# Neighbourhood attention in an encoder trunk: one unit of work per head instead of two

## The chip, the cores and the metric

The kernel runs on one core of one Trainium2 chip, in one launch. The metric is the device time of that launch in microseconds (us). The core's engines work side by side and each takes its own instructions strictly in order: PE does matrix products (its weight loads are listed apart as PEld), DVE does elementwise work and reductions, ACT does activation functions and scaled copies, POOL a few small powers and some transfers, SP issues nearly all DMA transfers. Products are written to PSUM, which has eight banks of 512 float32 columns for 128 partitions. Everything else lies in SBUF.

## The reference

The program computes two layers of an encoder trunk on one sequence of 512 tokens (8 rows by 64 columns of a grid) with 1024 features in float32. Each layer mixes tokens in three parallel ways, merges them with sigmoid gates, and follows with a SwiGLU block and a gated embedding. Only the third mixer is touched by the change:

```
def neighbourhood_attention(qc, kc, vc, rpb):          # 8 heads of 64 features
    R = S // GRID_W                                    # 8 rows, 64 columns
    cs = clip(cols - NA_KC // 2, 0, GRID_W - NA_KC)    # each query sees 16 columns ...
    col_idx = cs[:, None] + arange(NA_KC)[None, :]
    def row(args):
        ...                                            # ... of all 8 rows
        s = einsum('bhwd,bhrwcd->bhwrc', q_r, kn) * DC ** -0.5
        s = s + bias
        a = softmax(s.reshape(B, HC, GRID_W, KR * NA_KC), axis=-1)
        return einsum('bhwrc,bhrwcd->bhwd', a, vn)
```

## The kernel before

**Layout.** Tokens are reordered so that the eight rows of one grid column lie together. A block of 128 queries then needs only a short run of keys: the four query blocks of a head see the key runs `KEYS = ((0, 192), (64, 256), (192, 256), (320, 192))` (first key, count). What lies in a run but outside a query's window is masked by a bias of -1e30, which comes with the position bias as a ready table from memory.

**Precision.** Every float32 operand of a product is split into a high and a low part (`split`: an ACT copy gives the high part, a DVE subtraction the low one), and a plain product is issued three times (`mm3`, lines L178 to L180). Queries and keys of the neighbourhood heads are stacked so that two products per score tile are enough (L803). Probabilities are split after their transposition (lines of `split` with tile `pt` and `a`), and the value matrix already carries its high and low halves side by side in 128 columns per head, so a value product gives two halves of 64 rows that are added at the end.

**Order of the work.** PE's instructions run in the order in which the Python program emits them. The large projections are walked in chunks of three products of 512 columns; every fourth chunk calls `tick`, which resumes the small generators that wait (`live`) and starts at most one new one from a queue (`later`, with a delay and a gap before the next start). So a neighbourhood unit is cut by its `yield`s into steps, and each step is put between two groups of twelve wide products. The other engines' instructions are put in order by a scheduler from priorities; `high_priority(offset=n)` moves an instruction up by n places. Weights are loaded by SP into three buffers (`wr`, L172), split by ACT and DVE into `wh` and `wl`, and used by PE.

**A unit before.** `natten_in` makes queries and keys of two heads (`pr` is the pair) and queues four units: (half 0, head 0), (half 0, head 1), (half 1, head 0), (half 1, head 1), one tick apart. A unit (`natten_unit`) covers two of the four query blocks of one head:

1. One bias tile `b` of 128 by 2 by 256 is loaded by SP (L704, two buffers). Two score tiles of 192 and 256 columns are made in one PSUM bank each (L803, tag `sc`, two banks). DVE adds the bias, negates and takes the row minimum in one instruction that writes back into `b` (L713); ACT takes exponentials from `b` into a tile `e` with the row sum (tag `e`, four buffers); DVE takes reciprocals (L721); ACT scales both `e` tiles in place.
2. After two ticks PE transposes four blocks into one bank (L729, tag `tr`, two banks); three of them are split into `pt` (128 by 384), the fourth, which has 64 keys only, into `a`.
3. After two more ticks PE makes the value products: two of 256 columns (L743), two of 128 (L745), one of 128 (L746), in a bank with tag `av` for the first head and `mm` for the second. ACT and DVE split the result into `y` and add its halves.

The three projections `glu`, `diff` (the first mixer, differential attention, whose units use the same `sc`, `tr`, `av` banks and `e`, `pt`, `a` tiles) and `gatec` run between and after these units. `conv` taps fill DVE in the background.

Of the kernel before, what the change touches and what calls it, by code (L numbers as in the profile page):

```python
# [20 lines left out]
P = 128  # L21
L = 2
# [6 lines left out]
HC = 8  # L29
# [2 lines left out]
HALO = CON3W // 2  # L32
NA_KR = 8
NA_KC = 16
NW = 256
KEYS = ((0, 192), (64, 256), (192, 256), (320, 192))
PLE = 256
DFF = 2816
# [5 lines left out]
FILL = -1.0e30  # L44
# [8 lines left out]
ORDER = (0, 2, 4, 6, 1, 3, 5, 7)  # L53
GAP = 144
HIGH = 200
BACC = dict(dynamic_dma_scratch_size=1024)


# [4 lines left out]
class Net:  # L63
# [315 lines left out]
    def small(self):  # L379

        for tag in ("ident", "ones"):
            self.sb(tag, [P, P], bufs=1)
        for tag in ("onesr", "zeror"):
            self.sb(tag, [P, P], F32R, bufs=1)
        for tag, n in (("b", 2 * NW), ("s", 10), ("sm", 8), ("rc", 4)):
# [214 lines left out]
    def values(self, ap, parts):  # L600


        mm = self.nc.tensor.matmul
        accs = [self.ps("mm", (P, 2, 256)) for _ in range(2)]
        for o in range(0, KD, 4):
            wh, wl = self.weights(ap[:, o * 256:(o + 4) * 256], 1024)
            both = [(k, t) for k in range(o, o + 4) for t in range(4)]
            if o == 0:

                both.sort(key=lambda kt: kt[1] // 2)  # L610
            for n, (k, t) in enumerate(both):
# [6 lines left out]
                mm(out, self.h[k][:, 0, ts], wl[:, s], start=False, stop=False,  # L618
                   skip_group_check=True)
                mm(out, self.h[k][:, 1, ts], wh[:, s], start=False,  # L620
                   stop=k == KD - 1 and t % 2 == 1, skip_group_check=True)
                if n % 2:
                    self.chunk()
        vs = []
        for acc in accs:
            v = self.sb("v", [P, 2, 512], F32R)
            for t in range(2):
                for hi, lo, a in parts(v[:, t], acc[:, t]):
                    self.split(hi, lo, a)
            vs.append(v)  # L630
        return vs

    def natten_in(self, pr, st, ys):
# [63 lines left out]
    def natten_unit(self, pr, half, u, st4, k2, st, y):  # L697

        nc, i = self.nc, self.i
        mm = nc.tensor.matmul  # L700
        head = 2 * pr + u
        b = self.sb("b", [P, 2, NW])
        with self.tc.high_priority(offset=100):
            nc.sync.dma_start(b, self.a["bias"][i, head, half])  # L704
        es = []
        m = self.sb("s", [P, 6])
        for t in range(2):
            qt = 2 * half + t
            k0, n = KEYS[qt]
            sc = self.ps("sc", (P, n))  # L710
            self.scores(sc, st4, k2, u, slice(qt * P, (qt + 1) * P), slice(k0, k0 + n))
            with self.tc.high_priority(offset=min(HIGH, self.tc.cur_priority - self.p0)):
                nc.vector.tensor_tensor_reduce(  # L713
                    out=b[:, t, :n], in0=sc, in1=b[:, t, :n], scale=-1.0, scalar=3.0e38,
                    op0=ALU.add, op1=ALU.min, accum_out=m[:, t:t + 1])
            e = self.sb("e", [P, n])
            self.act(e, b[:, t, :n], AF.Exp, table="exp", scale=-1.0, bias=m[:, t:t + 1],
                     accum_out=m[:, 2 + t:3 + t])
            es.append(e)
        with self.tc.high_priority(offset=min(HIGH, self.tc.cur_priority - self.p0)):  # L720
            nc.vector.reciprocal(m[:, 4:6], m[:, 2:4])  # L721
        for t, e in enumerate(es):
            self.act(e, e, AF.Copy, scale=m[:, 4 + t:5 + t])
        yield 2
        pt = self.ps("tr", (P, 4, P))
        p2 = self.sb("a", [P, P], F32R)
        outer, inner = es[half], es[1 - half]
        near, far = (64, 0) if half == 0 else (0, P)
        turn = lambda out, a: nc.tensor.transpose(out, a, self.ident)  # L729
        turn(pt[:, half], outer[:, near:near + P])  # L730
        turn(pt[:, 1 - half], inner[:, half * P:half * P + P])
        turn(pt[:, 2], inner[:, P - half * P:2 * P - half * P])
        turn(pt[:64, 3], outer[:, far:far + 64])
        pp = self.sb("pt", [P, 2, 512], F32R)[:, :, :3 * P]
        self.split(pp[:, 0], pp[:, 1], pt[:, :3].rearrange("p a b -> p (a b)"))
        self.split(p2[:64], p2[64:], pt[:64, 3])
        yield 2
        vs = st["v"]
        av = self.ps(("av", "mm")[u], (P, 256))
        cols = slice(head * P, head * P + P)  # L740
        at = lambda t: slice(t * P, (t + 1) * P)
        for k in range(2):
            mm(av, vs[2 * half][:, cols], pp[:, k, :256], start=k == 0, stop=False)  # L743
        for k in range(2):
            mm(av[:, at(1 - half)], vs[1][:, cols], pp[:, k, 256:], start=False, stop=False)  # L745
        mm(av[:, at(half)], vs[3 + half][:, cols], p2, start=False, stop=True)  # L746


        qs = slice(half * 256, half * 256 + 256)
# [635 lines left out]
def _bias_tiles(rpb):  # L1385
    t = np.arange(S)
    w, r = t // GR, t % GR
    cs = np.clip(w - NA_KC // 2, 0, GW - NA_KC)
    out = np.full((L, HC, 4, P, NW), FILL, dtype=rpb.dtype)
    for qt in range(4):  # L1390
        q = np.arange(qt * P, (qt + 1) * P)
        k0, n = KEYS[qt]
        k = np.arange(n) + k0
        ro = r[k][None, :] - r[q][:, None] + NA_KR - 1
        co = w[k][None, :] - w[q][:, None] + NA_KC - 1
        ok = (w[k][None, :] >= cs[q][:, None]) & (w[k][None, :] < cs[q][:, None] + NA_KC)
        out[:, :, qt, :, :n] = np.where(
            ok, rpb[:, :, np.where(ok, ro, 0), np.where(ok, co, 0)], out[:, :, qt, :, :n])
    out = out.reshape(L, HC, 2, 2, P, NW).transpose(0, 1, 2, 4, 3, 5)
    return np.ascontiguousarray(out)  # L1400


# [7 lines left out]
def _layout(v):  # L1410
# [4 lines left out]
    for i in range(L):  # L1415
# [44 lines left out]
```

## Time and profile before

| | us |
|---|---|
| Median of three runs | 1774.33 (1773.85 to 1774.78) |
| Profiled execution, its own time | 1775.07 |
| Its span, first to last instruction | 1773.3 |
| PE busy | 1763.5 |
| PE weight loads busy | 1555.2 |
| DVE busy | 1420.0 |
| ACT busy | 891.2 |
| POOL busy | 98.4 |

The profile is of one execution. Its span lies 1.77 us under that execution's own time, and that time lies 0.74 us over the median. Products are pipelined and the end of each is modelled, so PE is shown busy nearly always; what PE really spends on a product is read from the distance between the starts of two successive products, which the timeline gives. A row such as `natten_e<-natten_b,natten_s 128x256 f32` names the tile written, the tiles read and the shape; a bracket at the end of a timeline row gives the idle time before the instruction and what ended it. The units of this change run in two stretches, from 79.8 us to about 180 us in the first layer and from 958.5 us to about 1060 us in the second.

### The profile page before, as it was taken

To read this page: it belongs to the slowest core of one execution; us is meant where nothing else is said; L and a number is where in the kernel's file an instruction comes from. 1 tells how busy PE (TensorE), PEld (TensorE's weight loads), DVE (VectorE), ACT (ScalarE), POOL (GpSimd) and SP (SyncE) were. 2 spreads that over 40 slices of the span, in tenths; PEclk is the share of its full clock that TensorE was granted. 3 is DMA by queue.
4 is the path that set the end of the run, shared out by engine and by line. 5 is a ranking of instruction groups with operands and counts; after the bars stand their busy time and mean duration, and the time that the engine had idled before them with its cause. 6 is when DMAs were issued, how large, how long until landed. Compare 5 with 4: busy or idle time off the path is not lost.

```text
span 1773.3 us, 27306 instructions
## 1 busy us (share of the span) xinstructions
PE 1763.5 (99%) x10178; PEld 1555.2 (88%) x10178; DVE 1420.0 (80%) x2418; ACT 891.2 (50%) x1561; POOL 98.4 (6%) x114
## 2 busy tenths in 40 slices
PE   9999999999999999999999999999999999999998
PEld 7888888888899899998888888888888998989987
DVE  7977987998798587787777779889887975867776
ACT  5576555225565254454545755452356643534444
POOL 0000000000111010100000000000001110101000
PEclk9999999999999999999999999999999999999999
DMA  5666541334757366544446755423256664656332
GB/s 207 171 192 172 161 125 43 113 99 140 228 152 189 115 166 160 136 125 128 139 127 188 189 155 149 113 72 96 92 176 201 173 179 113 176 136 159 99 104 95
DMA packets 112548, 255.00 MB, mean 144 GB/s; under 512 B 14368, under 2 KB 19232, under 8 KB 112416
## 3 DMA queue, kind: packets, MB, share of 16 engines
q1 hardware_dynamic: 99024, 228.88, 42.2%
q0 software_dynamic: 12672, 23.07, 8.2%
q8 instruction: 80, 1.31, 0.3%
q10 hardware_dynamic: 720, 1.31, 0.2%
q14 instruction: 52, 0.43, 0.1%
HBM read 215.46 MB, written 7.34 MB: 126 GB/s over the span
## 4 chain that ended last, share of the span: by engine, by line
PE 86%; DVE 6%; ACT 3%; DMA 3%; issue 1%; SPq 0%; POOL 0%; ACTq 0%; DVEq 0%; POOLq 0%
PE ffn_mm L1009 4%; PE ffn_mm L1011 4%; PE ffn_mm L178 4%; PE ffn_mm L179 4%; PE ffn_mm L180 4%; PE ffn_mm L1010 4%; PE ffn_sc L1011 3%; PE ffn_sc L1009 3%; PE ffn_sc L1010 3%; PE mergea_mm L178 2%; PE mergea_mm L180 2%; PE mergea_mm L179 2%; PE gateb_mm L179 2%; PE gateb_mm L178 2%; PE gateb_mm L180 2%; PE wo_mm L178 2%
## 5 line engine op out<-in xcount | busy, mean ns | idle before, releaser
L161 DVE SCALAR_TENSOR_TENSOR conv_z<-glu_z,pre_par,conv_z 128x512 f32<-128x512 f32 x240 | 179.5, 748 | 3.5
L144 ACT ACTIVATE ffn_wh<-ffn_wr 128x1024 fp32r<-128x1024 f32 (+1 forms) x92 | 92.7, 1014 | 111.4 <-PE ffn_mm L179 74.7
L979 POOL DMA_DIRECT2D ffn_qk<-w_fu x88 | 78.1, 989 | 604.8 <-DMA ffn_qk<-w_fu 368.2
L158 DVE TENSOR_TENSOR ffn_wl<-ffn_wr,ffn_wh 128x1024 fp32r<-128x1024 f32 (+1 forms) x92 | 107.3, 1172 | 5.4 <-ACT ffn_wh L144 4.9
L158 DVE TENSOR_TENSOR ffn_t<-ffn_mm,wo_rb 128x512 f32<-128x512 f32 (+1 forms) x64 | 38.6, 604 | 67.9 <-PE ffn_mm L180 67.9
L144 ACT ACTIVATE mergea_wh<-mergea_wr 128x1024 fp32r<-128x1024 f32 (+1 forms) x32 | 27.1, 846 | 96.8 <-PE mergea_mm L179 79.5
L144 ACT ACTIVATE ffn_wh<-ffn_qk 128x1024 fp32r<-128x1024 f32 x44 | 46.7, 1060 | 36.1 <-PE ffn_mm L179 16.0
L158 DVE TENSOR_TENSOR ffn_wl<-ffn_qk,ffn_wh 128x1024 fp32r<-128x1024 f32 x44 | 53.8, 1223 | 10.7 <-ACT ffn_wh L144 10.7
L158 DVE TENSOR_TENSOR ffn_t<-ffn_t,ffn_t 128x512 f32<-128x512 f32 (+1 forms) x46 | 31.3, 680 | 32.1 <-ACT ffn_t L144 31.5
L144 ACT ACTIVATE diff_a<-diff_sc,diff_s 128x512 f32<-128x512 f32 x32 | 22.0, 688 | 61.1 <-DVE diff_s L894 61.1
L178 PE MATMUL ffn_mm<-ffn_v,ffn_wh 128*128 128x512 f32 x132 | 51.4, 389 | 0.0
L179 PE MATMUL ffn_mm<-ffn_v,ffn_wh 128*128 128x512 f32 x132 | 51.4, 389 | 0.0
L180 PE MATMUL ffn_mm<-ffn_v,ffn_wl 128*128 128x512 f32 x132 | 51.3, 389 | 0.0
L178 PE MATMUL ffn_mm<-ffn_y,ffn_wh 128*128 128x512 f32 x132 | 51.3, 389 | 0.0
L179 PE MATMUL ffn_mm<-ffn_y,ffn_wh 128*128 128x512 f32 x132 | 51.3, 389 | 0.0
L180 PE MATMUL ffn_mm<-ffn_y,ffn_wl 128*128 128x512 f32 x132 | 51.3, 389 | 0.0
L1010 PE MATMUL ffn_sc<-wo_h,ffn_wh 128*128 128x256 f32 x176 | 49.8, 283 | 0.0
L1011 PE MATMUL ffn_sc<-wo_h,ffn_wl 128*128 128x256 f32 x176 | 49.8, 283 | 0.0
L1010 PE MATMUL ffn_mm<-wo_h,ffn_wh 128*128 128x256 f32 x176 | 49.8, 283 | 0.0
L1011 PE MATMUL ffn_mm<-wo_h,ffn_wl 128*128 128x256 f32 x176 | 49.8, 283 | 0.0
L1009 PE MATMUL ffn_sc<-wo_h,ffn_wh 128*128 128x256 f32 x176 | 49.8, 283 | 0.0
L1009 PE MATMUL ffn_mm<-wo_h,ffn_wh 128*128 128x256 f32 x176 | 49.8, 283 | 0.0
(879 smaller groups left out, 6569.4 us busy)
## 6 DMA issues: line engine op xcount, KB each, us to landing
ffn_qk<-w_fu POOLq DMA_DIRECT2D x88, 256.0 KB, 5.9
ffn_wr<-w_fg SPq DMA_DIRECT2D x44, 512.0 KB, 3.7
ffn_wr<-w_fd SPq DMA_DIRECT2D x32, 448.0 KB, 4.0
ffn_r<-w_fu SPq DMA_DIRECT2D x44, 256.0 KB, 4.0
ffn_qk<-w_fg SPq DMA_DIRECT2D x44, 256.0 KB, 4.3
ffn_qk<-w_fu SPq DMA_DIRECT2D x44, 256.0 KB, 4.5
natten_wr<-w_in SPq DMA_DIRECT2D x16, 512.0 KB, 4.3
natten_b<-bias SPq DMA_DIRECT2D x32, 256.0 KB, 4.0
```

The costliest lines, as they stand in the source:

```text
L144: i = self.nc.scalar.activation(out, in_, func, **kw)
L158: return self.nc.vector.tensor_tensor(out, a, b, op)
L161: return self.nc.vector.scalar_tensor_tensor(out, a, s, b, op0, op1)
L178: mm(out, wh, ah, start=first, stop=False)
L179: mm(out, wh, al, start=False, stop=False)
L180: mm(out, wl, ah, start=False, stop=last)
L979: nc.gpsimd.dma_start(q, wu[:, lo], accum_op=ALU.add)
L1009: mm(out, wh[:, c], bh, start=first and k == 0, stop=False, skip_group_check=True)
L1010: mm(out, wh[:, c], bl, start=False, stop=False, skip_group_check=True)
L1011: mm(out, wl[:, c], bh, start=False, stop=k == 3, skip_group_check=True)
```

## The change

A unit now covers a whole head. Two units per pair are queued instead of four, with a gap of two ticks.

- **Scores.** The two score tiles of a half share one bank of 448 columns (192 and 256). All four tiles' products of a head are emitted one half after the other, eight products in a row.
- **Softmax in place.** The bias tiles are now two per head, 128 by 448, held in the tags `e` and `b` by turns (six buffers in all). The exponentials and the scaled probabilities overwrite them; no separate `e` tile is used. One reciprocal serves all four tiles.
- **Transposes.** After `WAIT` = 3 ticks (2 before) eight transposes run in a row into both `tr` banks. Their splits are one of 128 by 512, one of 128 by 256 and one of 64 by 256, moved up by 20 places (`SOON`).
- **Values.** After `VALW` = 2 ticks: six products of 256 columns and two of 128, all into one bank of 512 columns. The middle value block, which before met each half in 128 columns, meets both halves at once (columns 128 to 384).
- **Result.** `y` is split and added in one pass of 512 columns instead of two of 256.

```
-        for n in range(4):
-            self.later(self.natten_unit(pr, n // 2, n % 2, st4, k2, st, ys[pr]), 6 if pr == 3 else 5 if pr else 11, 1)
+        for u in range(2):
+            self.later(self.natten_unit(pr, u, st4, k2, st, ys[pr]), 6 if pr == 3 else 5 if pr else 11, 2)
...
+        ahead = lambda: self.tc.high_priority(offset=min(HIGH, self.tc.cur_priority - self.p0))
+        sooner = lambda: self.tc.high_priority(offset=min(SOON, self.tc.cur_priority - self.p0))
+        bs = [self.sb(("e", "b", "e")[(2 * head + half) % 3], [P, NW]) for half in range(2)]
         with self.tc.high_priority(offset=100):
-            nc.sync.dma_start(b, self.a["bias"][i, head, half])
+            for half, b in enumerate(bs):
+                nc.sync.dma_start(b, self.a["bias"][i, head, half])
...
+        for half, b in enumerate(bs):
+            both = self.ps("sc", (P, NW))
+            ...
+                for a, keys in enumerate((st4[:, 2 + u], k2[:, u])):
+                    mm(both[:, c], st4[:, u, qt * P:(qt + 1) * P], keys[:, k0:k0 + n],
+                       start=t + a == 0, stop=a == 1, skip_group_check=True)
+            for qt, sc, e in parts:
+                with ahead():
+                    nc.vector.tensor_tensor_reduce(out=e, in0=sc, in1=e, ...)
+                self.act(e, e, AF.Exp, table="exp", scale=-1.0, bias=m[:, qt:qt + 1], ...)
+        with ahead():
+            nc.vector.reciprocal(m[:, 8:12], m[:, 4:8])
+        for qt, e in enumerate(es):
+            self.act(e, e, AF.Copy, scale=m[:, 8 + qt:9 + qt])
+        yield WAIT
...
+        turn(pt[:, 0], es[0][:, 64:192])
+        turn(pt[:, 1], es[1][:, :P])
+        turn(pt[:, 2], es[1][:, P:])
+        turn(pt[:, 3], es[2][:, :P])
+        p12 = self.sb("pt", [P, 2, 512], F32R)
+        with sooner():
+            self.split(p12[:, 0], p12[:, 1], pt.rearrange("p a b -> p (a b)"))
+        pt = self.ps("tr", (P, 4, P))
+        turn(pt[:, 0], es[2][:, P:])
+        turn(pt[:, 1], es[3][:, :P])
+        turn(pt[:64, 2], es[0][:, :64])
+        turn(pt[:64, 3], es[3][:, P:])
+        ...
+        with sooner():
+            self.split(p3[:, 0], p3[:, 1], pt[:, :256])
+            self.split(pe[:64], pe[64:], pt[:64, 256:])
+        yield VALW
...
         for k in range(2):
-            mm(av, vs[2 * half][:, cols], pp[:, k, :256], start=k == 0, stop=False)
+            values(slice(0, 256), vs[0], p12[:, k, :256], first=k == 0)
         for k in range(2):
-            mm(av[:, at(1 - half)], vs[1][:, cols], pp[:, k, 256:], start=False, stop=False)
-        mm(av[:, at(half)], vs[3 + half][:, cols], p2, start=False, stop=True)
+            values(slice(256, 512), vs[2], p3[:, k])
+        for k in range(2):
+            values(slice(128, 384), vs[1], p12[:, k, 256:])
+        values(at(0), vs[3], pe[:, :P])
+        values(at(3), vs[4], pe[:, P:], last=True)
...
-        self.split(y[rs, 0, qs], y[rs, 1, qs], av[rs])
-        self.tt(y[rs, 1, qs], y[rs, 1, qs].bitcast(F32), av[ro], ALU.add)
+        self.split(y[rs, 0], y[rs, 1], av[rs])
+        self.tt(y[rs, 1], y[rs, 1].bitcast(F32), av[ro], ALU.add)
```

The host's bias table is laid out to match (two tiles of 448 columns per head).

More of the change, by code (lines that the diff above doesn't have):

```diff
@@ L34 @@
 NA_KC = 16
-NW = 256
+NW = 448
 KEYS = ((0, 192), (64, 256), (192, 256), (320, 192))
@@ L55 @@
 HIGH = 200
+WAIT = 3
+SOON = 20
+VALW = 2
 BACC = dict(dynamic_dma_scratch_size=1024)
@@ L384, in small @@
             self.sb(tag, [P, P], F32R, bufs=1)
-        for tag, n in (("b", 2 * NW), ("s", 10), ("sm", 8), ("rc", 4)):
+        for tag, n in (("b", 512), ("s", 12), ("sm", 8), ("rc", 4)):
             self.sb(tag, [P, n])
@@ L695, in natten_v, with natten_unit @@
         st["v"] = [w.rearrange("p a b c -> p (a b c)") for w in (*vs, *ends)]
-    def natten_unit(self, pr, half, u, st4, k2, st, y):
+    def natten_unit(self, pr, u, st4, k2, st, y):
         nc, i = self.nc, self.i
@@ L705, in natten_unit @@
         es = []
[L706 to L724, printed above, removed]
-        pt = self.ps("tr", (P, 4, P))
[L726 to L739, printed above, removed]
@@ L740, in natten_unit @@
-        cols = slice(head * P, head * P + P)
-        at = lambda t: slice(t * P, (t + 1) * P)
+        m = self.sb("s", [P, 12])
+        for half, b in enumerate(bs):
+            both = self.ps("sc", (P, NW))
+            parts = []
+            for t in range(2):
+                qt = 2 * half + t
+                k0, n = KEYS[qt]
+                c = slice(0, n) if t == 0 else slice(NW - n, NW)
+                parts.append((qt, both[:, c], b[:, c]))
+                for a, keys in enumerate((st4[:, 2 + u], k2[:, u])):
[3 more added lines that the diff above has]
+                with ahead():
+                    nc.vector.tensor_tensor_reduce(
+                        out=e, in0=sc, in1=e, scale=-1.0, scalar=3.0e38,
+                        op0=ALU.add, op1=ALU.min, accum_out=m[:, qt:qt + 1])
+                self.act(e, e, AF.Exp, table="exp", scale=-1.0, bias=m[:, qt:qt + 1],
+                         accum_out=m[:, 4 + qt:5 + qt])
+                es.append(e)
@@ new lines, in natten_unit @@
+        with ahead():
[3 more added lines that the diff above has]
+        yield WAIT
+        at = lambda t: slice(t * P, (t + 1) * P)
+        turn = lambda out, a: nc.tensor.transpose(out, a, self.ident)
+        pt = self.ps("tr", (P, 4, P))
+        turn(pt[:, 0], es[0][:, 64:192])
+        turn(pt[:, 1], es[1][:, :P])
+        turn(pt[:, 2], es[1][:, P:])
+        turn(pt[:, 3], es[2][:, :P])
@@ new lines, in natten_unit @@
+        p12 = self.sb("pt", [P, 2, 512], F32R)
[6 more added lines that the diff above has]
+        turn(pt[:64, 3], es[3][:, P:])
+        pt = pt.rearrange("p a b -> p (a b)")
+        p3 = self.sb("pt", [P, 2, 256], F32R)
+        pe = self.sb("a", [P, 256], F32R)
+        with sooner():
+            self.split(p3[:, 0], p3[:, 1], pt[:, :256])
+            self.split(pe[:64], pe[64:], pt[:64, 256:])
@@ L742, in natten_unit, with values @@
+        yield VALW
+        vs = [v[:, head * P:head * P + P] for v in st["v"]]
+        av = self.ps(("av", "mm")[u])
+        def values(c, v, p, first=False, last=False):
+            mm(av[:, c], v, p, start=first, stop=last, skip_group_check=True)
         for k in range(2):
-            mm(av, vs[2 * half][:, cols], pp[:, k, :256], start=k == 0, stop=False)
+            values(slice(0, 256), vs[0], p12[:, k, :256], first=k == 0)
         for k in range(2):
-            mm(av[:, at(1 - half)], vs[1][:, cols], pp[:, k, 256:], start=False, stop=False)
@@ L746, in natten_unit @@
-        mm(av[:, at(half)], vs[3 + half][:, cols], p2, start=False, stop=True)
-        qs = slice(half * 256, half * 256 + 256)
+            values(slice(256, 512), vs[2], p3[:, k])
[3 more added lines that the diff above has]
+        values(at(3), vs[4], pe[:, P:], last=True)
         rs, ro = (slice(0, 64), slice(64, P))[::-1 if u else 1]
-        self.split(y[rs, 0, qs], y[rs, 1, qs], av[rs])
-        self.tt(y[rs, 1, qs], y[rs, 1, qs].bitcast(F32), av[ro], ALU.add)
+        self.split(y[rs, 0], y[rs, 1], av[rs])
@@ L1388, in _bias_tiles @@
     cs = np.clip(w - NA_KC // 2, 0, GW - NA_KC)
-    out = np.full((L, HC, 4, P, NW), FILL, dtype=rpb.dtype)
+    out = np.full((L, HC, 2, P, NW), FILL, dtype=rpb.dtype)
     for qt in range(4):
@@ L1396, in _bias_tiles @@
         ok = (w[k][None, :] >= cs[q][:, None]) & (w[k][None, :] < cs[q][:, None] + NA_KC)
-        out[:, :, qt, :, :n] = np.where(
-            ok, rpb[:, :, np.where(ok, ro, 0), np.where(ok, co, 0)], out[:, :, qt, :, :n])
-    out = out.reshape(L, HC, 2, 2, P, NW).transpose(0, 1, 2, 4, 3, 5)
+        part = out[:, :, qt // 2, :, NW - n if qt % 2 else 0:NW if qt % 2 else n]
+        part[...] = np.where(ok, rpb[:, :, np.where(ok, ro, 0), np.where(ok, co, 0)], part)
     return np.ascontiguousarray(out)
```

1 line of the change is left out of this document (removed).

## The prediction

> **What bounds the kernel now.** I read the page first: busy times, granted clock, the chain of waits.
>
> ```profile
> span 1773.3 us, 27306 instructions
> PE 1763.5 (99%) x10178; PEld 1555.2 (88%) x10178; DVE 1420.0 (80%) x2418; ACT 891.2 (50%) x1561; POOL 98.4 (6%) x114
> PEclk9999999999999999999999999999999999999999
> PE 86%; DVE 6%; ACT 3%; DMA 3%; issue 1%; SPq 0%; POOL 0%; ACTq 0%; DVEq 0%; POOLq 0%
> ```
>
> PE is never idle for long, at full clock, and makes up most of the chain. Whatever leaves PE's stream is won; what leaves DVE or ACT is won only where PE waits for them. A busy PE says nothing of its pace, so next comes the timeline of PE around the units: the first column is the start, and the distance between starts is what an instruction costs.
>
> ```profile
> 79.78 0.25 PE L803 MATMUL natten_sc<-natten_qk 128*128 128x192 f32 x1
> ...
> 80.25 0.40 PE L178 MATMUL natten_mm<-glu_h,natten_wh 128*128 128x512 f32 x1
> ...
> 93.28 0.39 PE L180 MATMUL natten_mm<-glu_h,natten_wl 128*128 128x512 f32 x1
> 93.51 0.40 PE L743 MATMUL natten_av<-natten_pt,natten_v 128*128 128x256 f32 x2
> 93.74 0.34 PE L745 MATMUL natten_av<-natten_pt,natten_v 128*128 128x128 f32 x2
> 93.92 0.28 PE L746 MATMUL natten_av<-natten_a,natten_x 128*128 128x128 f32 x1
> 94.03 0.63 PE L729 MATMUL natten_tr<-pre_ident,natten_e 128*128 128x128 f32 x4
> 94.41 0.48 PE L178 MATMUL natten_mm<-glu_h,natten_wh 128*128 128x512 f32 x1
> 94.73 0.39 PE L179 MATMUL natten_mm<-glu_h,natten_wh 128*128 128x512 f32 x1
> ```
>
> A wide product of 512 columns takes 0.23 us (93.28 to 93.51). Two value products of 256 take 0.23 together, two of 128 take 0.18, the last of 128 takes 0.11. So a narrow product costs nearly as much as one of twice its width; something other than its columns sets the price. The third thing to read is where PE's stream has holes in these units:
>
> ```profile
> 149.28 0.28 PE L618 MATMUL diff_mm<-diff_wl,glu_h 128*128 128x256 f32 x1
> 149.40 0.28 PE L620 MATMUL diff_mm<-diff_wh,glu_h 128*128 128x256 f32 x1
> 149.67 0.88 PE L743 MATMUL natten_mm<-natten_pt,natten_v 128*128 128x256 f32 x2
> ...
> 151.09 0.33 PE L746 MATMUL natten_mm<-natten_a,natten_x 128*128 128x128 f32 x1 [0.36 <-DVE natten_a L158]
> 151.30 0.33 PE L803 MATMUL natten_sc<-natten_qk 128*128 128x192 f32 x1
> ...
> 162.27 0.28 PE L803 MATMUL natten_sc<-natten_x,natten_qk 128*128 128x256 f32 x1
> 163.34 0.36 PE L803 MATMUL natten_sc<-natten_qk 128*128 128x192 f32 x1 [0.79 <-DVE natten_s L713]
> ...
> 1028.16 0.34 PE L745 MATMUL natten_mm<-natten_pt,natten_v 128*128 128x128 f32 x2
> 1028.77 0.33 PE L746 MATMUL natten_mm<-natten_a,natten_x 128*128 128x128 f32 x1 [0.27 <-DVE natten_a L158]
> ...
> 1040.13 0.28 PE L803 MATMUL natten_sc<-natten_x,natten_qk 128*128 128x256 f32 x1
> 1041.39 0.35 PE L803 MATMUL natten_sc<-natten_qk 128*128 128x192 f32 x1 [0.98 <-DVE natten_s L713]
> ```
>
> Against the undisturbed distances, the score waits cost 1.07 - 0.12 = 0.95 us and 1.26 - 0.12 = 1.14 us: a score tile waits for a bank that DVE has not yet read. The value waits cost 1.90 - 0.64 = 1.26 us (149.40 to 151.30, against 0.12 + 0.52) and 0.61 - 0.18 = 0.43 us: DVE splits the probabilities late. These four places, 3.8 us, are all the holes over 0.3 us that I find in the units' two stretches.
>
> **The change part by part.**
>
> *Value products.* Per head there were ten, 2 x 0.52 = 1.04 us. There will be six of 256 and two of 128. Dear case: six at the pace of the row pair 149.28 to 149.40 (0.12) and two at 0.11, 0.94 us. Cheap case: six at 0.115 (half of 0.23) and two at 0.09, 0.87 us. The gain is 0.10 to 0.17 us per head; I take 0.14, the middle, since both rows are of this very form. Over 16 heads: 2.2 us (1.6 to 2.7).
>
> *Transposes.* Eight before, eight after, but in one series. A series of four takes 0.38 us and makes the wide product behind it 0.32 instead of 0.23: 0.47. Eight in a row pay the 0.09 once: 0.85 instead of 0.94 at best, nothing at worst, since some series now stand before scores and not before wide products. I take 0.03 per head, 0.5 us in all (0 to 1.4).
>
> *Scores.* The same eight products; 0.47 us per four (79.78 to 80.25), zero change. Reading the first tile must now wait for the second one in its bank, under 0.47 us, hidden by the three ticks that follow.
>
> *The softmax chain.* Its prices, in the first layer's stretch:
>
> ```profile
> L144 ACT ACTIVATE natten_e<-natten_b,natten_s 128x256 f32<-128x256 f32 x16 | 8.0, 499 | 1.6 <-DVE natten_s L713 1.6
> L144 ACT ACTIVATE natten_e<-natten_e,natten_s 128x256 f32<-128x256 f32 x16 | 8.0, 502 | 1.1 <-DVE natten_s L721 0.9
> L144 ACT ACTIVATION_READ_ACCUMULATOR natten_e<-natten_b,natten_s 128x1 f32 x32 | 6.0, 188 | 0.0
> L713 DVE CUSTOM_DVE_ANT_0 natten_b<-natten_sc,natten_b 128x256 f32<-128x256 f32 x16 | 6.7, 419 | 2.7 <-DMA natten_b<-bias 2.6
> 90.63 0.27 PE L803 MATMUL natten_sc<-natten_x,natten_qk 128*128 128x192 f32 x1
> 96.73 0.85 ACT L144 ACTIVATE natten_e<-natten_e,natten_s 128x256 f32<-128x256 f32 x2
> 97.77 0.63 PE L729 MATMUL natten_tr<-pre_ident,natten_e 128*128 128x128 f32 x4
> ```
>
> The unit of 90.63 is the tightest: its scaled copies end at 97.58, its transposes start at 97.77. With four tiles the chain grows by at most two exponentials with their sum reads, 2 x (0.50 + 0.19), and two copies, 0.85: 2.2 us, so 6.95 becomes 9.2 us. The allowance grows from two ticks to three; a tick is twelve wide products, 2.7 us, and the 7.14 us between 90.63 and 97.77 becomes 9.9 us with the same other steps between. The cover holds by about 0.7 us in the worst place and by more elsewhere. If it is gone, PE waits for copies at every head that is late: that is the slower rival below. The rows exclude a gain here.
>
> *The score waits.* A head took four banks in two steps one tick apart; now it takes the two banks once, and the next head comes two ticks later. At 162.27 the bank asked for belonged to the unit of the tick before. What DVE has to do in it doubles (two more reads of about 0.42 us), but the time for it grows by 2.7 us. I let both waits go: 2.1 us (0 to 2.1).
>
> *The value waits.* The splits behind the transposes become wider, 512 columns in one bank, then 256 and 64 by 256 in the other, instead of 384 and 64 by 128 twice, still with two ticks.
>
> ```profile
> L158 DVE TENSOR_TENSOR natten_pt<-natten_tr,natten_pt 128x384 fp32r<-128x384 f32 x16 | 8.9, 554 | 0.7 <-ACT natten_pt L144 0.5
> L144 ACT ACTIVATE natten_a<-natten_tr 64x128 fp32r<-64x128 f32 x16 | 4.3, 268 | 7.2 <-DVE natten_pt L158 6.9
> SPq L704 <- ACT natten_e L144: 20.9, 14, 4.5
> ```
>
> A split that comes late on an engine working in order stands behind other work, so moving it up by 20 places helps; a chain that handles 512 columns at a time instead of 384, and needs a second bank, hurts. Bounds: 1.7 us better to 2 us worse; I take 0.4 us better, since such a step is late in only two of 32 units.
>
> *Bias tiles.* 32 loads as before, with fewer columns. SP's queue stood 20.9 us behind loads whose tile the exponentials had not left. Now a tile is free after the transposes of three heads before, some six ticks earlier than it is used. What is queued behind on SP is weights; PE shows no wait for them, so I count zero. ACT and DVE lose instructions (one reciprocal instead of two, five splits instead of six); zero too, as neither bounds.
>
> *New waits.* A rearranged stream that was nearly free of holes will get some. No row shows them; at worst 0.5 us at each of 16 heads, 8 us; I take 0.8 us, two holes of the size seen.
>
> **Sum:** -2.2 - 0.5 - 2.1 - 0.4 + 0.8 = -4.4 us. On the profiled execution, 1773.3 of span and 1.77 around it, 1775.07 becomes 1770.7; the median lies 0.74 lower, so I forecast **1769.9 us**.
>
> **The rivals.**
>
> *By columns alone: no difference.* Streamed columns do not change: 2 x (2 x 256 + 3 x 128) = 1792 before, 6 x 256 + 2 x 128 = 1792 after. At the wide product's pace that is 0.80 us per head both times, and the 2.2 us vanish: 1772.1 us. Against it stands the measured 1.04. [...]
>
> *The waits only move: no difference.* PE's 2.7 us are won, but new holes match the old 3.8: 1774.3 - 2.7 + 0.8 = 1772.4 us. For it: DVE's lateness comes from the other work on it in these ticks, which stays.
>
> *The softmax is late: slower.* Four tiles in series on ACT miss the third tick where ACT also has weight splits and a table load, and DVE, in order, stands at the single reciprocal with weight splits queued behind it. It decides when the chain exceeds 9.9 us after the last score, against 9.2 worked out. If half of the 16 heads are late by 1 us: 1774.3 - 2.7 + 8 = 1779.6 us. For it: a margin of 0.19 us at one unit before. Against it: most units had more than 1 us.
>
> **How the numbers follow.** A measurement of this kernel can tell about 0.2%, 3.5 us, from no change: faster means below 1770.8, slower above 1777.9. Forecast 0.52; columns alone 0.08 and moved waits 0.20, both "same"; late softmax 0.20. So faster 0.52, same 0.28, slower 0.20. For the range: all holes gone and the cheap prices give 1774.3 - 2.7 - 1.4 - 3.8 = 1766.4, so the low end is 1766.5; the high end reaches into the slower case, 1779. The likeliest case's own range is 1766.5 to 1771.5.
>
> **What would show it.** Right: eight value products of a head in 0.87 to 0.94 us; eight transposes in 0.75 to 0.85; no score product waiting for L713; PE holes in the units' stretches of about 2 us in sum, and copies that end before their transposes start. Wrong: transposes whose releaser is ACT's scaled copy, value products that wait for the split of `pt` or `a` at more than two heads, eight value products that take 1.0 us or more, or a difference that lies outside these two stretches.

## The result and the profile after

| | median us (range, executions) | ratio to before, 95% interval |
|---|---|---|
| Before, timed beside it | 1773.83 (1773.58 to 1774.78, 8) | 1 |
| After | 1768.73 (1767.87 to 1770.24, 8) | 0.9972 (0.9961 to 0.9983) |
| After, timed again in another set | 1769.04 (1767.39 to 1770.31, 7) | 0.9972 (0.9961 to 0.9982) |

The change makes the kernel 5.1 us faster; 1769.9 was forecast. The profiled execution after took 1768.34 us, 6.7 less than the profiled one before: that one lay 1.24 above its median, this one 0.39 below. The parts below are of the profiled executions. Two rows of the page after, whose span is 1766.6 us:

```profile
PE 1759.3 (100%) x10146; PEld 1551.8 (88%) x10146; DVE 1408.6 (80%) x2354; ACT 885.5 (50%) x1529; POOL 98.4 (6%) x114
PE 92%; DVE 4%; DMA 2%; ACT 2%; issue 1%; SPq 0%; POOL 0%; ACTq 0%; POOLq 0%; DVEq 0%
```

PE's share of the chain of waits rose from 86% to 92%: less of the end is now set by PE waiting for DVE and ACT. Where the time came from is seen from marks that are the same in both kernels. First before, then after: the first score products of the second layer's units and the first merge products of both layers. The numbers behind the colon are least, median and greatest duration in ns, then the first and last start in us.

```profile
L178 PE MATMUL mergea_mm<-glu_h,mergea_wh x64: 389/389/389, 333.3 to 395.1; 128*128 128x512 f32 x64
L803 PE MATMUL natten_sc<-natten_qk x8: 249/280/365, 958.5 to 969.3; 128*128 128x192 f32 x4, 128*128 128x256 f32 x4
L178 PE MATMUL mergea_mm<-ple_h,mergea_wh x64: 389/389/389, 1211.5 to 1273.3; 128*128 128x512 f32 x64
```

```profile
L181 PE MATMUL mergea_mm<-glu_h,mergea_wh x64: 389/389/389, 329.7 to 391.6; 128*128 128x512 f32 x64
L722 PE MATMUL natten_sc<-natten_qk x8: 249/266/306, 955.0 to 962.1; 128*128 128x192 f32 x4, 128*128 128x256 f32 x4
L181 PE MATMUL mergea_mm<-ple_h,mergea_wh x64: 389/389/389, 1204.7 to 1266.6; 128*128 128x512 f32 x64
```

The new kernel is ahead by 3.6 us at the first merge, still by 3.5 us when the second layer's units begin, and by 6.8 us at the second merge. Nearly all of it is won in the two stretches with the units. The timeline of PE there, after:

```profile
96.22 0.87 PE L763 MATMUL natten_av<-natten_pt,natten_v 128*128 128x256 f32 x6
97.41 0.44 PE L763 MATMUL natten_av<-natten_a,natten_x 128*128 128x128 f32 x2 [0.31 <-DVE natten_a L161]
97.68 1.06 PE L738 MATMUL natten_tr<-pre_ident,natten_e 128*128 128x128 f32 x8
98.50 0.48 PE L181 MATMUL natten_mm<-glu_h,natten_wh 128*128 128x512 f32 x1
98.82 0.40 PE L182 MATMUL natten_mm<-glu_h,natten_wh 128*128 128x512 f32 x1
...
105.08 0.88 PE L763 MATMUL natten_mm<-natten_pt,natten_v 128*128 128x256 f32 x6
105.79 0.34 PE L763 MATMUL natten_mm<-natten_a,natten_x 128*128 128x128 f32 x2
105.97 0.45 PE L181 MATMUL glu_mm<-glu_h,glu_wh 128*128 128x512 f32 x1
...
148.44 0.88 PE L763 MATMUL natten_mm<-natten_pt,natten_v 128*128 128x256 f32 x6
149.33 0.30 PE L722 MATMUL natten_sc<-natten_qk 128*128 128x192 f32 x1
150.28 0.30 PE L619 MATMUL diff_mm<-diff_wh,glu_h 128*128 128x256 f32 x1
```

The eight value products of a head take 0.89 us (105.08 to 105.97, and 148.44 to 149.33). The eight scores of a head take 0.95 us without a wait (149.33 to 150.28), where two units before waited for L713. The one value wait left is at 97.41: 1.19 us for six products that take 0.71 elsewhere, so the hole is 0.48. The split of `a` that it waits for stands behind a table load on ACT, as ACT's timeline shows:

```profile
94.75 1.28 ACT L147 ACT_TABLE_LOAD   x1
...
96.54 0.37 ACT L147 ACTIVATE natten_a<-natten_tr 64x256 fp32r<-64x256 f32 x1
```

For the whole account I added up the distances between successive starts on PE, by the kind of the earlier instruction, over both stretches (from 75 us and from 903.5 us to the first merge product; after, the same instructions). In us, before and after: score products 24.45 and 20.15, transposes 11.92 and 12.87, value products 18.23 and 14.98, wide products into `mm` 386.24 and 387.26, differential scores 31.96 and 31.09, products of 256 columns into `mm` 46.52 and 46.33, all others equal. The sum is 566.01 and 559.37: 6.64 us less. With the single holes taken out, read from the timelines:

| term | forecast | measured |
|---|---|---|
| value products, pace alone | -2.2 | -2.0 |
| transposes, scores and the wide products beside them, pace alone | -0.5 | -0.7 |
| score waits | -2.1 | -2.1 |
| value waits of before | -0.4 | -1.7 |
| new waits (0.48 at 97.41, 0.25 at 174.18, 0.17 at 1048.74) | +0.8 | +0.9 |
| differential scores and other products | 0 | -1.1 |
| sum (of the unrounded terms) | -4.4 | -6.6 |

### The profile page after: what moved, and what is told of

The parts are those of the page before. It is cut to its first block, busy times and chain, and to the rows that moved or that the text cites. A ratio compares the mean times of both kernels' runs of the same rounds, so it can differ in the third digit from the quotient of the medians.

```text
span 1766.6 us, 27127 instructions
## 1 busy us (share of the span) xinstructions
PE 1759.3 (100%) x10146; PEld 1551.8 (88%) x10146; DVE 1408.6 (80%) x2354; ACT 885.5 (50%) x1529; POOL 98.4 (6%) x114
## 4 chain that ended last, share of the span: by engine, by line
PE 92%; DVE 4%; DMA 2%; ACT 2%; issue 1%; SPq 0%; POOL 0%; ACTq 0%; POOLq 0%; DVEq 0%
PE ffn_mm L1034 4%; PE ffn_mm L1036 4%; PE ffn_mm L182 4%; PE ffn_mm L181 4%; PE ffn_mm L183 4%; PE ffn_mm L1035 4%; PE ffn_sc L1036 3%; PE ffn_sc L1034 3%; PE ffn_sc L1035 3%; PE mergea_mm L182 2%; PE mergea_mm L183 2%; PE mergea_mm L181 2%; PE gateb_mm L182 2%; PE gateb_mm L183 2%; PE gateb_mm L181 2%; PE wo_mm L182 2%
## 5 line engine op out<-in xcount | busy, mean ns | idle before, releaser
L147 ACT ACTIVATE natten_e<-natten_e,natten_s 128x192 f32<-128x192 f32 (+1 forms) x88 | 39.3, 474 | 25.2 <-DVE natten_s L726 21.9
L1035 PE MATMUL ffn_mm<-wo_h,ffn_wh 128*128 128x256 f32 x176 | 49.8, 283 | 0.0
```

What stands on the lines that cost most here:

```text
L147: i = self.nc.scalar.activation(out, in_, func, **kw)
L1035: mm(out, wh[:, c], bl, start=False, stop=False, skip_group_check=True)
```

## The experiments

**The value products.** Two kernels issue the same columns in more products. The first cuts the middle block, ten products per head as before the change:

```
-            values(slice(128, 384), vs[1], p12[:, k, 256:])
+            values(slice(128, 256), vs[1], p12[:, k, 256:384])
+            values(slice(256, 384), vs[1], p12[:, k, 384:])
```

> The changed kernel with only the middle value block cut back into 128 columns: four products where the change has two of 256, so ten value products per head as in the kernel before, all else as changed. If the price of a narrow product is its weight load (about 0.11 us whatever its width), a head's value products go from 0.89 to about 1.04 us, 16 x 0.15 = 2.4 us: 1771.1 us (1770.5 to 1772.0). If the columns set the price, as the rival has it: 1768.7 to 1768.9. If the whole gain came from waits: also no difference.

The second cuts the outer blocks `vs[0]` and `vs[2]` in the same way too, fourteen products per head.

> The suspected cost magnified: all six value products of 256 columns cut into twelve of 128, fourteen products per head. By weight loads: six more at 0.10 to 0.11 us, 16 x 0.63 = 10 us: 1778.5 us (1777 to 1780). By columns: 1768.7 to 1769.0.

Measured: 1778.37 us (1776.14 to 1780.0), ratio 1.0024 (1.0015 to 1.0033), and 1791.35 us (1790.11 to 1791.97), ratio 1.0098 (1.0083 to 1.0114). PE's timeline of the same head, first the one, then the other (a merged row shows one shape only; the first eight products are four of 256 and four of 128 columns):

```profile
104.96 1.03 PE L763 MATMUL natten_mm<-natten_pt,natten_v 128*128 128x256 f32 x8
...
106.06 0.45 PE L181 MATMUL glu_mm<-glu_h,glu_wh 128*128 128x512 f32 x1
...
1055.97 0.39 PE L829 MATMUL diff_sc<-diff_x,diff_qk 128*128 128x512 f32 x1
1058.82 0.50 PE L829 MATMUL diff_sc<-diff_qk 128*128 128x512 f32 x1 [2.47 <-ACT diff_e L147]
```

```profile
105.76 1.45 PE L763 MATMUL natten_mm<-natten_pt,natten_v 128*128 128x128 f32 x12
...
107.27 0.44 PE L181 MATMUL glu_mm<-glu_h,glu_wh 128*128 128x512 f32 x1
```

Eight, ten and fourteen products take 0.89, 1.10 and 1.51 us for the same 1792 columns: 0.10 us per product more, 3.4 and 9.9 us over 16 heads. The rival of the columns falls. (The ten products of before, in two series of five, took 1.04 us; no run explains the 0.06 us between that and 1.10.) But the kernels lose 9.3 and 22.3 us against the 1769.04 of the changed kernel beside them. The rest is holes that the changed kernel lacks, and slow products behind some of them (last section): 2.6 us at 1055.97 above, 1.7 us at 177.5, 0.7 us each at 149.85 and 1028.29 in the first; in the second, 2.7 us and 2.8 us where a value product waits for a bank that ACT's rope step (`diff_rp`) has not yet read, and 1.3 us more before the differential scores behind each of the two. Only PE products were changed, yet in the first kernel's trace 90 of 1529 instructions on ACT and 130 of 2354 on DVE (told apart by operation, tiles and shape) stand at other places in their engine's order than after the change, while the two traces of the changed kernel have the same order: the scheduler has ordered those engines anew. So the time of such a run is not that of the edit alone, and the pace of a series has to be read from the starts.

**The score waits.** In the kernel before, the two score tiles of a unit share one bank, so that all four products stand ahead of the two reads; nothing else is edited:

```
+        both = self.ps("sc", (P, 448))
...
-            sc = self.ps("sc", (P, n))
-            self.scores(sc, st4, k2, u, slice(qt * P, (qt + 1) * P), slice(k0, k0 + n))
+            c = slice(0, n) if t == 0 else slice(448 - n, 448)
+            ...                               # both tiles' four products first, then the two reads
```

> The kernel before, half heads and all, with one thing of the change: a unit's two score tiles share one bank, so that a bank is asked for again two units later instead of one. If the score waits come from the bank, they go: 1773.8 - 2.1 = 1771.7 us (1771 to 1773), with no score product waiting for L713's reads and the value waits as before. Rival: the spacing of the units decides, not the bank, or the waits only move to the transposes: 1773.8 us.

Measured: 1780.32 us (1779.12 to 1780.81), ratio 1.0034 (1.0021 to 1.0046). The longest hole on PE's timeline, and the longest row of PE's waits (total us, times, longest):

```profile
1052.31 0.39 PE L180 MATMUL diff_mm<-ple_h,diff_wl 128*128 128x512 f32 x1
1054.38 0.50 PE L749 MATMUL natten_mm<-natten_pt,natten_v 128*128 128x256 f32 x2 [1.68 <-ACT diff_rp L144]
```

```profile
PE natten_mm L749 <- ACT diff_rp L144: 2.4, 2, 1.7
```

No score waits for L713 any more, and the holes have moved: values wait for banks and for splits, transposes for copies. They sum to 9.7 us against 3.8. In this half-head form the rival "the waits only move" holds, and worse.

The other way round, the changed kernel with its units one tick apart (`11, 1)` for `11, 2)` in the two-unit queue) should bring the score waits back, if my reason for their going (more time between units) were right:

> The changed kernel with the second head of a pair one tick after the first instead of two. Both score banks are then asked for 2.7 us after they were filled, and DVE's four reads took 2 to 4 us in the kernel before, so the second head's scores wait at most pairs by 0.5 to 1.5 us: 8 x 1 = 8 us, 1776 us (1771 to 1780). If the spacing was not what removed the score waits: 1768.7 us.

Measured: 1787.16 us (1786.73 to 1787.8), ratio 1.0072 (1.0057 to 1.0087), 18 us over the changed kernel. PE's timeline and the longest row of its waits:

```profile
118.59 0.27 PE L738 MATMUL natten_tr<-pre_ident,natten_b 128*128 128x128 f32 x1
119.49 0.41 PE L738 MATMUL natten_tr<-pre_ident,natten_b 128*128 128x128 f32 x2 [0.63 <-DVE natten_a L161]
```

```profile
PE natten_tr L738 <- DVE natten_a L161: 4.6, 8, 0.9
```

The scores still wait nowhere: eight in 0.90 to 0.96 us at every head. What waits is the second head's transposes, for the two `tr` banks that the first head holds until its splits have read them; by the distances between starts this costs some 8.5 us. Value products that wait for splits cost 3.1 us, and two holes of 2.4 us before wide products, with the slow products behind one of them, 6.4 us. That is the 18 us. So the two ticks are needed, but not for the scores. What made the score waits before is seen in DVE's timeline of the kernel before, around the first of them:

```profile
161.18 0.41 DVE L713 CUSTOM_DVE_ANT_0 natten_b<-natten_sc,natten_b 128x256 f32<-128x256 f32 x1
161.79 1.23 DVE L158 TENSOR_TENSOR gatec_wl<-gatec_wr,gatec_wh 128x1024 fp32r<-128x1024 f32 x1 [0.18 <-ACT gatec_wh L144]
162.93 0.35 DVE L713 CUSTOM_DVE_ANT_0 natten_b<-natten_sc,natten_b 128x192 f32<-128x192 f32 x1
```

A weight split of 1.23 us stood between the two reads of a unit, and the score of 163.34 waited for the second. With a shared bank these waits are gone in all three kernels seen, units of two tiles one tick apart and whole heads one and two ticks apart. The time between does not explain it: at one tick apart a bank is asked for again 3.7 us later, as in the kernel before (158.42 and 162.07). Whether the bank itself ends the waits or the timing of DVE against PE that comes with it is not told apart; the run with the splits moved up in the kernel before, below, shows that the timing alone can end most of them.

**The third tick.** `WAIT` = 2 for 3, which leaves the four-tile softmax the time that two tiles had before:

> The changed kernel with two ticks instead of three between a head's scores and its transposes. The slower rival's mechanism, made to happen: four tiles in series on ACT need 2.2 us more than two, and before only a few units had that much to spare. If the chain is as worked out, transposes wait for the scaled copies by 0.3 to 2 us at most heads: 16 x 0.5 = 8 us, 1776 us (1772 to 1782). If the chain is shorter than worked out: 1768.7 us, and the third tick was cover for nothing.

Measured: 1770.57 us (1769.88 to 1771.52), ratio 0.9979 (0.997 to 0.9988). The row of PE's waits at the transposes:

```profile
PE natten_tr L738 <- ACT natten_e L147: 0.2, 1, 0.2
```

The view of waits shows one wait of the transposes, 0.2 us, but the starts show more. ACT's timeline and PE's at one head:

```profile
108.71 0.86 ACT L147 ACTIVATE natten_b<-natten_b,natten_s 128x192 f32<-128x192 f32 x2 [0.32 <-DVE natten_s L733]
109.48 0.84 ACT L147 ACTIVATE natten_e<-natten_e,natten_s 128x256 f32<-128x256 f32 x2
```

```profile
109.22 0.84 PE L738 MATMUL natten_tr<-pre_ident,natten_b 128*128 128x128 f32 x3
110.02 0.68 PE L738 MATMUL natten_tr<-pre_ident,natten_e 128*128 128x128 f32 x3
110.67 0.34 PE L722 MATMUL natten_sc<-natten_qk 128*128 128x192 f32 x1
```

The copies still run while the transposes do, and the eight transposes take 1.45 us (109.22 to 110.67) instead of the 0.79 of the changed kernel. Three heads have 1.45 us and one has 1.23, 2.4 us in all. So the slower rival's mechanism is real at two ticks, at four of 16 heads, and the third tick is what keeps it away; its price is 2.4 us and not 8. Two waits for a bank, 0.9 us each, are new as well. The chain ends 5.5 to 7.4 us after the last score's start, where I had worked out 9.2.

The changed kernel was not timed again beside this run. Against its two sets above the tick is worth 1.5 to 1.8 us, and 1.2 to 1.5 us if each is taken against the kernel before beside it (1774.2 here); the intervals of the ratios overlap.

**The splits moved up.** `SOON` = 0 for 20:

> The changed kernel without moving the splits of the transposed probabilities up by 20 places; PE's order is the same. If the move is what ended the value waits of the kernel before (1.7 us at two places), they come back: 1770.5 us (1769.5 to 1772), in the stretch where the diff projections begin. If the whole-head shape ended them: 1768.7 us.

Measured: 1770.21 us (1769.28 to 1770.88), ratio 0.9977 (0.9968 to 0.9987). The value waits are back, as PE's timeline shows for one of three places:

```profile
1024.94 0.88 PE L763 MATMUL natten_mm<-natten_pt,natten_v 128*128 128x256 f32 x6
1026.45 0.44 PE L763 MATMUL natten_mm<-natten_a,natten_x 128*128 128x128 f32 x2 [0.63 <-DVE natten_a L161]
```

That is 1.51 - 0.71 = 0.8 us here, 1.0 us at 97 and 0.5 us at 150.6. So in the whole-head form the 20 places end two of the three value waits and halve the one at 97. They do not do so alone: the same move in the kernel before,

```
+        with self.tc.high_priority(offset=min(20, self.tc.cur_priority - self.p0)):
+            self.split(pp[:, 0], pp[:, 1], pt[:, :3].rearrange("p a b -> p (a b)"))
+            self.split(p2[:64], p2[64:], pt[:64, 3])
```

> The kernel before with the splits of the transposed probabilities moved up by 20 places, the one scheduling aid of the change that fits half-head units; PE's order is the same. If that move alone ends the value waits (1.7 us where the diff projections begin), 1772.3 us (1771.5 to 1773), with the two score waits (2.1 us) left as they are. If the aid works only with the whole-head spacing, or the order on ACT and DVE merely shifts the holes: 1773.8 us or more.

gave 1776.03 us (1775.11 to 1777.08) beside 1775.0 of before, ratio 1.0006 (0.9997 to 1.0015): no gain. On PE's timeline the waits stand earlier, before the first value product instead of before the later ones, here for a bank from which DVE had yet to add `y`:

```profile
1028.48 0.28 PE L620 MATMUL diff_mm<-diff_wh,ple_h 128*128 128x256 f32 x1
1029.77 0.48 PE L744 MATMUL natten_mm<-natten_pt,natten_v 128*128 128x256 f32 x2 [1.01 <-DVE natten_y L158]
```

Four such places cost 1.2 us each (149.35, 169.66, 1028.48, 1048.69). The score waits, whose two banks are as before, shrink from 2.1 us to 0.4 us (163.05 - 162.71 - 0.12 = 0.22 at the first, 0.23 at the second): DVE makes the second read 0.3 us earlier and PE asks 0.4 us later than before. "The waits only move" describes this kernel. And more of the move in the changed kernel, `SOON` = 60, which I tried as a version that might beat it:

> The changed kernel with the splits moved up by 60 places instead of 20, meant to beat it: the one value wait left in its profile (0.5 us at 97 us, behind a sigmoid with its table load) should go: 1768.3 us (1767.5 to 1769). Rival: the splits now push weight splits back and PE waits there: 1769.5 to 1772 us.

gave 1770.22 us (1769.27 to 1772.31), ratio 0.9975 (0.9965 to 0.9986), 4.8 us under the kernel before beside it, as the changed kernel is: no difference can be told. The hole at 97 stays at 0.46 us, and PE waits elsewhere: 1.4 us each at 177.76 and 1053.46, where differential scores wait for ACT's `diff_e`.

**Exponentials in the bias tiles.** The changed kernel with two bias tiles in the tag `b` and the exponentials in four tiles `e` of their own:

```
-        bs = [self.sb(("e", "b", "e")[(2 * head + half) % 3], [P, NW]) for half in range(2)]
+        bs = [self.sb("b", [P, NW]) for half in range(2)]
...
-                self.act(e, e, AF.Exp, table="exp", scale=-1.0, ...)
+                b, e = e, self.sb("e", [P, KEYS[qt][1]])
+                self.act(e, b, AF.Exp, table="exp", scale=-1.0, ...)
```

> The changed kernel with the exponentials in tiles of their own again: bias tiles in two buffers of tag b, exponentials in four of tag e, as before, so that one head fills all of both. The next head's exponentials, two ticks later, must then wait for the first head's transposes at three ticks: its copies come late by up to 1.5 us at eight heads, and the bias loads hold SP's queue: 1776 us (1770 to 1785). If keeping them in the bias tiles was worth nothing: 1768.7 us.

Measured: 1775.24 us (1773.33 to 1777.23), ratio 1.0005 (0.9996 to 1.0015). As expected, the exponentials of the second head of each pair start only behind the first head's transposes: at these eight heads that is 3.5 to 3.9 us after the last score's start, against 0.6 to 2.6 us in the changed kernel. But their copies still end 2.0 us or more before their transposes start, and PE waits for none of them. The loss is two waits of value products for a split, here the first on PE's timeline, with PE's window after it (length, then busy us and count of PE, PEld, DVE, ACT, POOL, then the granted clock, DMA's share and GB/s):

```profile
96.50 0.76 PE L764 MATMUL natten_av<-natten_pt,natten_v 128*128 128x256 f32 x5
99.78 0.44 PE L764 MATMUL natten_av<-natten_a,natten_x 128*128 128x128 f32 x2 [2.52 <-DVE natten_a L161]
```

```profile
100.50:104.00 3.50, 3.50 (x14) 2.82 (x13) 3.24 (x6) 2.47 (x5) 0.00 (x0) 0.59 0.91 252
```

At 975.87 there is another of 2.7 us, and behind both the clock fell, to 0.59 as in the window above and to 0.52 from 978.40 to 981.90. DVE's timeline shows what the split of `a` stood behind:

```profile
98.05 1.23 DVE L161 TENSOR_TENSOR natten_wl<-natten_wr,natten_wh 128x1024 fp32r<-128x1024 f32 x1 [2.43 <-ACT natten_wh L147]
99.30 0.42 DVE L161 TENSOR_TENSOR natten_a<-natten_tr,natten_a 64x256 fp32r<-64x256 f32 x1
```

A weight split stands ahead of the split of `a` on DVE, and on ACT too (`natten_wh` at 96.97, `natten_a` at 97.92). In the changed kernel it stands behind on both: on ACT `natten_a` comes at 96.54 and `natten_wh` at 96.80, on DVE `natten_a` at 96.94 and `natten_wl` at 97.88. So the tiles of their own cost 6.2 to 6.5 us against the two sets of the changed kernel (5.8 to 6.1 if each is taken against the kernel before beside it), by another order on ACT and DVE. Why the scheduler chose that order was not followed further.

**The changed kernel again.** It was profiled a second time:

> The changed kernel again, as the base of the comparisons beside it: 1768.7 us, 0.997 of the kernel before, with holes over 0.15 us in PE's stream of at most 1.5 us in the two stretches.

That execution took 1770.31 us, 2 us more than the first. PE's timeline, then DVE's:

```profile
157.49 0.28 PE L722 MATMUL natten_sc<-natten_x,natten_qk 128*128 128x192 f32 x1
159.04 0.47 PE L181 MATMUL diff_mm<-glu_h,diff_wh 128*128 128x512 f32 x1 [1.27 <-DVE natten_y L161]
```

```profile
152.21 0.69 DVE L161 TENSOR_TENSOR diff_rp<-diff_rp,diff_r 128x512 f32<-128x512 f32 x1 [2.56 <-DMA diff_rp<-diff_rp]
```

A hole of 1.44 us (1.55 less the 0.11 of a score product) that the first execution does not have. DVE had waited 2.56 us for a transfer of the rope step, and the addition of `y` that frees the bank stood behind it in DVE's order. The holes over 0.15 us sum to 2.5 us in this execution, where I had expected 1.5 at most. The profile with `SOON` = 60 has a hole of 1.3 us at the same place, released by the same addition. In the pair of profiles this hole accounts for most of the 2 us between them, not necessarily for all of the spread of 1767.4 to 1770.3.

## Why the prediction was right, and where its steps were not

The forecast sum was 4.4 us, the account of the two profiled executions gives 6.6 and the medians 5.1. The terms were not all right: value waits and terms that were not named brought 2.4 us more than forecast, and that the median came within 1.2 us of 1769.9 is in part luck.

**Value products.** Right in mechanism and nearly in size: 0.89 us per head, within the 0.87 to 0.94 named, and 2.0 to 2.4 us in all (the whole account, or 0.15 at 16 heads). The kernels with more and narrower products show that their number is what costs, 0.10 us for each one more.

**Transposes.** The series of eight with the wide product behind it takes less than two of four: 98.50 - 97.68 = 0.82, and 0.09 on the next, 0.91 against 0.94 at that head. With the scores and the wide products 0.7 us were won, 0.5 forecast.

**Score waits.** They went, 2.1 us as forecast, but the reason that I gave, 2.7 us more between the units, was not it: at one tick apart they do not come back. What ended them stays open.

**The softmax chain.** This step was mis-sized, without harm. I added the whole of the new work, 2.2 us, to the longest of the 32 units, 6.95 us, and got 9.2. Measured the same way, from the last score's start to the end of the copies, the units before took 3.5 to 6.95 us, 5.0 on average; the heads after took 5.5 to 7.8 us, 6.9 on average. So the average grew by 1.9 us, but the longest by 0.9. The unit that I took already held a table load and, behind it, a sigmoid of another projection of 0.60 us, as ACT's timeline before shows:

```profile
94.78 1.28 ACT L144 ACT_TABLE_LOAD   x1
```

At the same place after, the table load of 94.75 stands behind the copies. The copies end at least 2.1 us before their transposes start, where I had left 0.7. The second execution after has one chain of 8.95 us, at the head of 156.70, where DVE had stood still for a transfer; it too ends 2.1 us or more ahead. At two ticks the cover is gone at four heads, so the rival was no idle one, but 20% on it, with 8 us as its price, was too much.

**Value waits.** The term that was mis-sized most: -0.4 forecast, -1.7 measured, with 0.48 of the new waits of the same kind. I had taken the worth of the 20 places as nearly cancelled by the wider chain. Without them the waits come back in three places, 2.3 us in sum, and the kernel is 1.2 to 1.5 us slower against the two sets of the changed kernel (0.8 to 1.1 if each is taken against the kernel before beside it).

**Bias tiles.** I counted the tiles used in place at zero, on the ground that PE did not wait for what stands behind the loads on SP. SP's wait for the exponentials did shrink as I had read it, from 20.9 us to 0.8. This is the larger of two rows after, then the row of the kernel with own tiles, where it is back:

```profile
SPq L710 <- ACT natten_b L147: 0.6, 1, 0.6
```

```profile
SPq L710 <- ACT natten_e L147: 20.0, 16, 5.7
```

But the choice of tiles is worth some 6 us, by the two waits of value products for DVE's split and the slower clock behind them (0.59 and 0.52).

**New waits, and what was not named.** 0.9 us for 0.8. The 1.1 us at the differential scores and products of 256 columns were not in the sum: two waits of about 0.4 us at 192.5 and 1070.8 went, a new one of 0.2 us stands at 1056.98, and the rest are small changes of pace; their cause was not looked for.

**The rivals.** The columns alone fall. The late softmax does not show at three ticks and costs 2.4 us at two. "The waits only move" came true in two kernels (one bank before the change, splits moved up before the change) and not in this one. What stays open is why just this order of ACT and DVE has so few holes. The runs give what single parts are worth in it (two ticks of gap 18 us, tiles in place some 6 us, third tick and moved splits 1 to 2 us each), but no rule by which it could have been foreseen that the edits to its parts lose and the whole wins; none of the variants beat it, though `SOON` = 60 is not told apart from it.

## What to carry to other kernels

Where narrow products each load their own weights, as here (10146 loads for 10146 products; each narrow one more cost 0.10 us, of which no run tells the load's part), price the series by its count, from the starts of a like series, and merge neighbours that share a weight block until the bank is full. Where the other engines' order is made by a scheduler, expect every edit to move waits of some us as well: read the gain of the edit from the starts of the instructions touched, and the rest from a list of holes. And take a chain's growth from all of its instances: the longest one may already hold other work of its engines. Last, a view of waits can miss what a series of short products loses between its members (0.2 us in the view against 2.4 us by the starts with two ticks); the distances between the starts do not.

## What the runs showed of the hardware

**The clock fell behind some holes of 2.4 us and more.** Wide products in a series run at 0.23 us each. After the hole of 2.6 us at 1055.97 in the kernel with ten products, seven of them ran at 0.43 us and the next at 0.36, with a granted clock of 0.59 from 1058.60 to 1062.30; behind the first hole of 2.7 us in the kernel with own tiles the granted clock was 0.59 over 3.5 us, as shown there. In the executions whose longest holes were 1.44 us (the changed kernel again) and 1.84 us (the kernel before with one bank) the mean granted clock was 1.0. At 2.4 us it went either way: the kernel with one tick of gap has that hole in both layers, before 181.9 and before 1064.4, and the windows behind them differ above all in the granted clock (the columns are those of the window above):

```profile
181.60:185.10 3.50, 3.18 (x14) 2.63 (x15) 3.44 (x7) 1.92 (x5) 0.00 (x0) 1.00 0.65 193
1064.20:1067.70 3.50, 3.34 (x8) 2.67 (x9) 3.44 (x7) 1.76 (x5) 0.00 (x0) 0.54 0.71 198
```

Fourteen products in the one, eight in the other: the hole before 1064.4 cost some 1.6 us more than itself, by my estimate from eight products at the 0.43 us seen above in place of 0.23. The drops shown here came after holes of 2.4 to 2.7 us, 2.2 to 2.5 us of them idle by the profile. The length alone does not decide, as the pair above shows, and what else does is open.
